# Eight experts on one core: a 64-column expert instead of a 128-column one behind the alternating pair

## The chip, the cores and the metric

The kernel runs on one core of one Trainium2 chip, as one launch. The metric is the device time of a run in microseconds (us). The kernel before was timed in three runs; one more execution was profiled, and all rows below are from that one.

## The reference

Two decoder layers over 256 positions of width 1024, all in float32. The first layer has a dense feed-forward part; the second, which this change is about, sends every position to 2 of 8 experts:

```
logits = x @ router_w                      # 256 x 8
top_val, top_idx = top_k(logits, 2)
comb = softmax(top_val), scattered to 8 columns
for e in range(8):
    h = silu(x @ w_gate[e]) * (x @ w_up[e])            # 1024 -> 3584
    y += comb[:, e:e+1] * (h @ w_down[e])              # 3584 -> 1024
x = layer_norm(ALPHA * x + y)
```

Each expert's three matrices are 1024 x 3584 (twice) and 3584 x 1024 in float32, 44 MB; all eight are read.

## The kernel before, in words

**Columns and positions.** The kernel doesn't run all 256 positions through each expert. It gathers an expert's positions with a one-hot matmul into a few columns (`start_expert`), and scatters the result back with the transposed one-hot (`finish_expert`). The experts come in eight *places*, called positions here, 0 to 7. Position 0 is expert 0 with 128 columns. The other seven experts are ranked at run time by how many positions chose them (rank 0 has most), and `SEQ[s]` says which rank comes at position s, `CAP[s]` how many columns it gets there: 128 for ranks 0 and 1, 64 for the others. What doesn't fit is done by a loop at the end that is skipped when nothing is left over. SyncE reads the expert's number from a register for each weight transfer, so the order is fixed in the program and the experts are chosen by data.

**Two kinds of expert.** `CAP[s] == P` decides how the weights are used (`moe_unit`, `moe_project`, `down_block`):
- A *wide* expert (128 columns): each weight unit is split after arrival into a high half by ScalarE (L125) and a low half by VectorE (L143), each into a ring of three buffers, and TensorE makes three float32r matmuls for each float32 product. The raw unit's buffer is free as soon as the low half is written.
- A *small* expert (64 columns): TensorE reads the raw float32 unit, with two groups of 64 columns side by side in the array. The raw unit's buffer is free when those matmuls are done (`U.done`).

**Blocks.** An expert has seven blocks of 512 hidden units. A block is two units for gate, two for up, and later two for down, of 1 MB each. `moe_project` makes gate, ScalarE applies silu (L1232), `moe_project` makes up, VectorE multiplies (L1242). The down projection of a block comes after the up projection of the next one, so gate, up and the earlier block's down share the stream's order. Positions 0 and 1 (wide and small) alternate block by block and are the *pair*; its last two blocks are (1,5) and (1,6), both small. From position 2 on the experts come one after the other. (2,0) is block 0 of position 2.

```
blocks = [(0, 0), (0, 1), (0, 2), (1, 0), (1, 1)]
blocks += [x for b in range(3, NB) for x in ((0, b), (1, b - 1))] + [(1, NB - 1)]
blocks += [(s, b) for s in range(2, E) for b in range(NB)]
```

**The stream.** All weights go through `WeightStream`, in the order of use, on SyncE's DMA queue (L104). A unit's transfer is issued when a buffer comes free (`_fill`, `_freed`); there are fourteen for raw units in this part (five from the start, four added, three tiles of the mixer, two taken from the rings). `U.next` and `U.raw` also start the splitting of wide units up to two units ahead (`LOOK = 2`).

Of the kernel before, what the change touches and what calls it, by code (L numbers as in the profile page):

```python
# [35 lines left out]
        "P10": 10, "P11": 0, "vt": 4, "Lh": 5, "Ll": 6, "PTa0": 7, "PTa1": 3, "O": 10, "Ah": 2, "Al": 1,  # L36
        "xT0": 6, "xT1": 7, "setup": 9, "xf0": 0, "xf1": 9}
NM2 = 3
SEQ = (None, 3, 0, 4, 1, 5, 2, 6)
CAP = (128, 64, 128, 64, 128, 64, 64, 64)  # L40
NW_BASE = 5
NW_EXTRA = 4
LOOK = 2
# [155 lines left out]
def trunk(ctx, tc, x, xT, w_in, w_out, prm, wbd, rb, ohc, cst, ln1_g, ln1_b, ln2_g, ln2_b,  # L199
# [77 lines left out]
    def moe_unit(w, s, b, half, k):  # L277
        def src():
# [3 lines left out]
            return w[ds(e, 1), b, half].rearrange("o p (k n) -> p (o k) n", k=k)  # L282
        units.append((src, (k, 2048 // k), None, CAP[s] == P))

# [759 lines left out]
    def one_hot(pool, posc, name, T=P, bufs=1):  # L1044
        oh = pool.tile([P, 2, P // T, T], F32, name=name, tag="oh", bufs=bufs)
        for t in range(2):
            V.tensor_scalar(oh[:, t], iota[:, None, 0:T].to_broadcast([P, P // T, T]), posc(t), None,
                            op0=ALU.is_equal)
        return oh

    def gather(oh, dst, T=P):
        n = 512 // T
        for q in range(KC // n):
            p = sm()[:, 0:n * T].rearrange("p (a b) -> p a b", a=n)
            for j in range(n):
                k = q * n + j
                for t in range(2):
                    mm(p[:, j, :], xt[t][:, k * P:(k + 1) * P], oh[:, t, 0, :], t == 0, t == 1)
            dst(slice(q * n, q * n + n), p)
# [30 lines left out]
    def expert_one_hot(s):  # L1090
        ohe[s] = one_hot(ep, lambda t: (pos if s == 0 else posq)[:, t, s:s + 1], f"oh{s}", CAP[s], 2)

    def start_expert(s):
        wide = CAP[s] == P
        g = [ep.tile([P, KC, CAP[s]], F32R if wide else F32, name=f"g{s}_{i}", tag="g", bufs=3)
             for i in range(1 + wide)]

        def dst(a, p):
            A.activation(g[0][:, a, :], p, AF.Copy)
            if wide:  # L1100
                V.tensor_tensor(out=g[1][:, a, :], in0=p, in1=g[0][:, a, :].bitcast(F32), op=ALU.subtract)  # L1101

        gather(ohe[s], dst, CAP[s])
        st[s] = g

    def moe_project(s, g, between=None):
        T_ = CAP[s]
        C = P // T_
        n = 512 // C
        p = sm()[:, 0:n]  # L1110
        for kh in range(2):
            if C == 1:
                wh, wl = U.next()
            else:
                i, w = U.raw()
            if kh == 1 and between is not None:
                between()
            for k in range(4):
                kk = kh * 4 + k
                if C == 1:  # L1120
                    mm(p, g[0][:, kk, :], wh[:, k, :], kk == 0, False)
                    mm(p, g[0][:, kk, :], wl[:, k, :], False, False)
                    mm(p, g[1][:, kk, :], wh[:, k, :], False, kk == KC - 1)
                    continue
                for c in range(C):
                    mm(p[c * T_:(c + 1) * T_, :], g[0][:, kk, :], w[:, k, c * n:(c + 1) * n], kk == 0, kk == KC - 1)
            if C > 1:
                U.done(i)
        return p
# [48 lines left out]
    def route_ranks():  # L1178
# [8 lines left out]
        for s in range(1, E):  # L1187
            V.tensor_scalar(perm[:, s - 1, :], rank7, float(SEQ[s]), None, op0=ALU.is_equal)
        V.tensor_scalar(id7, iota[:, 1:E], UNSEL, None, op0=ALU.add)
# [259 lines left out]
```

## Time and profile before

| | us |
|---|---|
| median of three runs | 1282.12 (1280.95 to 1283.67) |
| the profiled execution, device time | 1284.04 |
| its span, first to last instruction | 1282.3 |
| TensorE busy | 1224.8 |
| VectorE busy | 647.4 |
| ScalarE busy | 518.1 |

The span and the busy times come from the profile of one execution. A busy TensorE is not one at its peak, since the ends of pipelined matmuls are modelled. Engines: PE is TensorE (PEld its weight loads), DVE VectorE, ACT ScalarE, POOL GpSimd, SP SyncE, whose queue (SPq) issues the weight transfers. A row of a table of stretches gives the stretch, its length, the busy time (and instructions) of PE, PEld, DVE, ACT and POOL, the granted TensorE clock (1.00 is full), the busy share of the DMA engines, and GB/s. A row of the timeline gives start, duration, engine, line, operation, and in brackets the idle time before it and what ended it. A row of instructions of one tile gives durations in ns (least, median, most) and the first and last start in us. The experts of the second layer run from about 420 us to the end.

### The profile page before, as it was taken

Reading aid. Unit: us, or ns where it says so; the run is one execution under the profiler, and the core shown is the slowest. Engines: PE = TensorE matmul, PEld = TensorE weight load, DVE = VectorE, ACT = ScalarE, POOL = GpSimd, SP = SyncE. Lnnn points to the kernel's source line nnn. Section 1 sums busy time; section 2 is a strip of 40 time slices with the busy share of each in tenths; the row PEclk is TensorE's granted clock in tenths of the full one; section 3 lists DMA queues with packets and bytes.
Section 4 is the critical chain, followed back from the end, with each engine's and each line's share of the span. In section 5 each row is a group of like instructions: output and inputs, shape, how many; then the busy total and the mean of one; then the engine's idle time right before and its main releaser. Section 6 shows DMA issues by size and latency. Waiting matters only on the chain. (4 is left out here: it accounts for less than half of the span.)

```text
span 1282.3 us, 18541 instructions
## 1 busy us (share of the span) xinstructions
PE 1224.8 (96%) x7564; PEld 911.7 (71%) x7564; DVE 647.4 (50%) x616; ACT 518.1 (40%) x549; POOL 81.0 (6%) x75
## 2 busy tenths in 40 slices
PE   9999999999999899999999999999999999799884
PEld 8979999999987776666678875568886554354441
DVE  6597544457688753445588841069882001001004
ACT  5674443344683542444467731057762000000001
POOL 3124000004022010000000000000000000000001
PEclk9999999999999999999999999999999999999998
DMA  9843545554377769999999979999999999999994
GB/s 350 310 176 143 208 176 196 198 213 150 149 285 276 272 249 415 420 421 420 421 420 414 367 278 420 420 420 421 421 421 392 420 420 421 420 420 420 421 420 180
DMA packets 63506, 428.99 MB, mean 335 GB/s; under 512 B 7951, under 2 KB 8376, under 8 KB 12984
## 3 DMA queue, kind: packets, MB, share of 16 engines
q1 hardware_dynamic: 62408, 423.55, 81.8%
q0 software_dynamic: 720, 3.68, 0.8%
q8 instruction: 61, 1.00, 0.3%
q10 hardware_dynamic: 288, 0.52, 0.1%
q14 instruction: 29, 0.24, 0.0%
HBM read 426.67 MB, written 2.63 MB: 335 GB/s over the span
## 5 line engine op out<-in xcount | busy, mean ns | idle before, releaser
L143 DVE TENSOR_TENSOR lo<-w,hi 128x2048 fp32r<-128x2048 f32 (+1 forms) x181 | 402.6, 2242 | 88.5 <-ACT hi L125 87.4
L125 ACT ACTIVATE hi<-w 128x2048 fp32r<-128x2048 f32 (+1 forms) x183 | 340.6, 1875 | 92.3 <-PE sm L240 52.8
L240 PE MATMUL sm<-w,g 128*64 128x256 f32 x2240 | 265.8, 382 | 4.3 <-DMA w<-in_moe_w_up_dram 4.2
L240 PEld LDWEIGHTS sm<-w,g 128*64 128x64 f32 x2240 | 159.2, 137 | 100.2 <-issue 23.7
L240 PE MATMUL sm<-hi,g 128*128 128x512 f32 x672 | 220.8, 400 | 1.5 <-DVE g L1101 1.5
L1242 DVE TENSOR_TENSOR h<-h,sm 128x256 f32<-128x256 f32 (+1 forms) x56 | 29.0, 518 | 294.7 <-PE sm L240 290.3
L240 PE MATMUL acc<-w,ht 128*64 128x512 f32 x560 | 141.5, 603 | 20.3 <-DMA w<-in_moe_w_down_dram 19.7
L1140 ACT ACTIVATE ht<-sm 128x256 f32<-128x256 f32 (+1 forms) x56 | 25.6, 457 | 322.4 <-PE sm L1138 322.4
L240 PEld LDWEIGHTS sm<-hi,g 128*128 128x128 f32 x672 | 126.7, 189 | 33.4 <-DVE g L1101 2.0
L240 PE MATMUL sm<-lo,g 128*128 128x512 f32 x336 | 133.7, 398 | 3.3 <-DVE lo L143 3.3
L240 PE MATMUL sm<-xh,hi 128*128 128x256 f32 x528 | 132.5, 284 | 0.0
L240 PE MATMUL sm<-xl,hi 128*128 128x256 f32 x528 | 132.0, 283 | 0.0
L240 PEld LDWEIGHTS acc<-w,ht 128*64 128x64 f32 x560 | 40.8, 138 | 99.2 <-issue 70.3
L240 PE MATMUL acc<-hi,ht 128*128 128x512 f32 x336 | 109.8, 398 | 0.0
L240 PEld LDWEIGHTS sm<-xh,hi 128*128 128x128 f32 x528 | 99.6, 189 | 1.7 <-issue 1.3
L240 PEld LDWEIGHTS sm<-xl,hi 128*128 128x128 f32 x528 | 99.8, 189 | 0.4
L240 PE MATMUL sm<-xh,lo 128*128 128x256 f32 x528 | 84.8, 283 | 0.0
L240 PEld LDWEIGHTS sm<-lo,g 128*128 128x128 f32 x336 | 63.5, 189 | 18.4 <-DVE lo L143 4.3
L240 PEld LDWEIGHTS acc<-hi,ht 128*128 128x128 f32 x336 | 63.0, 187 | 17.3 <-issue 2.7
L240 PEld LDWEIGHTS sm<-xh,lo 128*128 128x128 f32 x528 | 72.3, 189 | 0.0
L240 PE MATMUL acc<-lo,ht 128*128 128x512 f32 x168 | 67.1, 400 | 5.1 <-DVE lo L143 5.1
L353 POOL TENSOR_TENSOR mv<-mv,mhalf 128x1 f32<-128x1 f32 x8 | 7.0, 877 | 815.4 <-DVE mv L352 815.4
(263 smaller groups left out, 1177.7 us busy)
## 6 DMA issues: line engine op xcount, KB each, us to landing
w<-in_moe_w_gate_dram SPq DMA_DIRECT2D x112, 1024.0 KB, 13.7
w<-in_moe_w_up_dram SPq DMA_DIRECT2D x112, 1024.0 KB, 14.3
w<-in_moe_w_down_dram SPq DMA_DIRECT2D x110, 1024.0 KB, 15.7
w<-in_w_in_dram SPq DMA_DIRECT2D x18, 1024.0 KB, 6.1
w<-in_ffn_w_gate_dram SPq DMA_DIRECT2D x11, 1024.0 KB, 4.8
w<-in_ffn_w_up_dram SPq DMA_DIRECT2D x11, 1024.0 KB, 5.7
w<-in_ffn_w_down_dram SPq DMA_DIRECT2D x11, 1024.0 KB, 6.1
w<-in_w_out_dram SPq DMA_DIRECT2D x8, 1024.0 KB, 4.8
```

The source lines that it names most:

```text
L125: self.nc.scalar.activation(hi[a], w[a], AF.Copy)
L143: V.tensor_tensor(out=lo[a], in0=w[a], in1=hi[a].bitcast(F32), op=ALU.subtract)
L240: T.matmul(o, l, r, start=first, stop=last)
L353: G.tensor_tensor(out=o, in0=o, in1=mhalf, op=ALU.pow)
L1140: A.activation(ht[0], p[:, 0:nj, :], AF.Copy)
L1242: V.tensor_tensor(out=h, in0=h, in1=pu, op=ALU.mult)
```

## The change

Two of the constants at the head of the kernel are edited. Positions 0, 1, 6 and 7 keep their ranks; positions 2 to 5 hold ranks 4, 0, 5, 1 (64, 128, 64, 128 columns) where they held ranks 0, 4, 1, 5 (128, 64, 128, 64 columns). No other line changes.

```
-SEQ = (None, 3, 0, 4, 1, 5, 2, 6)
-CAP = (128, 64, 128, 64, 128, 64, 64, 64)
+SEQ = (None, 3, 4, 0, 5, 1, 2, 6)
+CAP = (128, 64, 64, 128, 64, 128, 64, 64)
```

## Rows read from the trace of the kernel before

**Rows 1.** The page: GB/s in 40 equal slices; the largest group of DMA issues.

```profile
GB/s 350 310 176 143 208 176 196 198 213 150 149 285 276 272 249 415 420 421 420 421 420 414 367 278 420 420 420 421 421 421 392 420 420 421 420 420 420 421 420 180
...
w<-in_moe_w_gate_dram SPq DMA_DIRECT2D x112, 1024.0 KB, 13.7
```

**Rows 2.** Busy times by stretch: the pair; the small experts at positions 6 and 7.

```profile
500.00:640.00 140.00, 137.09 (x777) 92.83 (x777) 69.81 (x50) 58.77 (x50) 0.00 (x0) 1.00 1.01 420
...
1062.00:1250.00 188.00, 166.44 (x1100) 84.27 (x1098) 15.17 (x30) 12.98 (x31) 0.00 (x0) 0.99 1.01 420
```

**Rows 3.** Busy times by stretches of 20 us, the five below 400 GB/s.

```profile
700.00:720.00 20.00, 20.00 (x90) 16.10 (x89) 17.13 (x9) 14.40 (x9) 0.00 (x0) 1.00 0.97 379
720.00:740.00 20.00, 20.00 (x92) 16.16 (x91) 17.16 (x9) 14.39 (x10) 0.00 (x0) 1.00 0.96 366
740.00:760.00 20.00, 20.00 (x120) 15.82 (x120) 8.77 (x6) 6.00 (x7) 0.00 (x0) 1.00 0.64 241
760.00:780.00 20.00, 19.27 (x136) 12.52 (x134) 8.09 (x9) 5.95 (x7) 0.00 (x0) 1.00 0.93 378
...
960.00:980.00 20.00, 19.27 (x128) 14.09 (x128) 6.47 (x6) 5.18 (x5) 0.00 (x0) 1.00 0.94 374
```

**Rows 4.** Waits of SyncE's queue, 710 to 785 us: total us, times, longest.

```profile
SPq L104 <- DVE lo L143: 36.0, 15, 4.0
SPq L104 <- PE sm L240: 16.2, 5, 9.0
```

**Rows 5.** Issue and landing of the last up unit of (1,6), (3,6), (7,4).

```profile
L104 SPq DMA_DIRECT2D w<-in_moe_w_up_dram x1: 333/333/333, 586.2 to 586.2; - x1
...
DMA to landing us min/median/max: 16.5/16.5/16.5
...
L104 SPq DMA_DIRECT2D w<-in_moe_w_up_dram x1: 332/332/332, 810.2 to 810.2; - x1
...
DMA to landing us min/median/max: 18.2/18.2/18.2
...
L104 SPq DMA_DIRECT2D w<-in_moe_w_up_dram x1: 333/333/333, 1201.6 to 1201.6; - x1
...
DMA to landing us min/median/max: 19.8/19.8/19.8
```

**Rows 6.** Timeline of VectorE: the product of gate and up in ten blocks.

```profile
623.29 0.42 DVE L1242 TENSOR_TENSOR h<-h,sm 128x256 f32<-128x256 f32 x1 [2.00 <-PE sm L240]
...
748.28 0.68 DVE L1242 TENSOR_TENSOR h<-h,sm 128x512 f32<-128x512 f32 x1
...
767.07 0.41 DVE L1242 TENSOR_TENSOR h<-h,sm 128x256 f32<-128x256 f32 x1
...
835.42 0.42 DVE L1242 TENSOR_TENSOR h<-h,sm 128x256 f32<-128x256 f32 x1 [10.44 <-PE sm L240]
...
855.43 0.69 DVE L1242 TENSOR_TENSOR h<-h,sm 128x512 f32<-128x512 f32 x1 [4.44 <-ACT hi L125]
...
960.27 0.68 DVE L1242 TENSOR_TENSOR h<-h,sm 128x512 f32<-128x512 f32 x1
...
979.06 0.41 DVE L1242 TENSOR_TENSOR h<-h,sm 128x256 f32<-128x256 f32 x1
...
1047.38 0.42 DVE L1242 TENSOR_TENSOR h<-h,sm 128x256 f32<-128x256 f32 x1 [10.44 <-PE sm L240]
...
1062.10 0.42 DVE L1242 TENSOR_TENSOR h<-h,sm 128x256 f32<-128x256 f32 x1 [14.30 <-PE sm L240]
...
1223.47 0.42 DVE L1242 TENSOR_TENSOR h<-h,sm 128x256 f32<-128x256 f32 x1 [7.53 <-PE sm L240]
```

**Rows 7.** Groups by line and shape: the split of a wide unit (busy, mean ns).

```profile
L143 DVE TENSOR_TENSOR lo<-w,hi 128x2048 fp32r<-128x2048 f32 x175 | 397.3, 2289 | 86.2 <-ACT hi L125 85.2
L125 ACT ACTIVATE hi<-w 128x2048 fp32r<-128x2048 f32 x177 | 335.9, 1913 | 90.0 <-PE sm L240 52.8 <-PE acc L240 26.9 <-ACT hi L125 4.7
```

**Rows 8.** Busy times and granted clock, 1226 to 1230 us.

```profile
1226.00:1230.00 4.00, 3.61 (x10) 1.15 (x12) 0.00 (x0) 0.00 (x0) 0.00 (x0) 0.57 1.02 424
```

## The prediction

> **What bounds the kernel now.** I read the page's line of transfer rates first. From about 500 us to the end the weights of the experts arrive at 420 GB/s, slice after slice, and only three slices fall clearly below it: 367, 278 and, later, 392 [rows 1]. A block of an expert takes six units of 1024 KB [rows 1], 6.29 MB, so the stream needs 14.95 us for a block at 421 GB/s. The table by stages says that two different things go on under the same rate. From 500 to 640 us TensorE is busy 137.1 of 140 us, so it only just keeps step. From 1062 to 1250 us it is busy 166.4 of 188 us at the same 420 GB/s: it has caught up and waits for weights [rows 2]. The end of the kernel is therefore set by the stream: time is won only where the stream itself stands still, or after its last unit.
>
> Where does it stand still? In four windows from 700 to 780 us it moves 379, 366, 241 and 378 GB/s, and 374 in the window 960 to 980 [rows 3]. Against 420.5 the first four are short by 41.5, 54.5, 179.5 and 42.5, together 318 GB/s over 20 us, or 318 / 420.5 x 20 = 15.1 us of stream time. The last is short by 46.5, or 2.2 us. Sum 17.3 us. The list of waits of the issuing queue says why: from 710 to 785 us it waits 36.0 us for low halves on VectorE and 16.2 us for matmuls, once 9.0 us [rows 4]. Both are the last readers of a weight buffer. No buffer is free, because TensorE is too far behind the stream.
>
> **How far behind, block by block.** I call *lag* the time from the arrival of a block's fourth unit (the last of gate and up) to the product of gate and up on VectorE (L1242). Arrivals are issue plus time to landing [rows 5], products are in [rows 6].
> The last block of the pair: 623.29 - (586.2 + 16.5) = 20.6 us.
> The last block of position 3: 835.42 - (810.2 + 18.2) = 7.0 us.
> A block that has caught up: 1223.47 - (1201.6 + 19.8) = 2.1 us, which is the floor.
> A block changes the lag by its own duration less 14.95 us of stream:
> - A wide expert behind a small one: from 835.42 to 960.27, 124.85 us for seven blocks, less 104.65, adds 20.2 us.
> - The first small block behind a wide one (it carries the wide expert's last down projection): 979.06 - 960.27 = 18.79 (767.07 - 748.28 at the first place is the same), adds 3.8 us.
> - The six other blocks of a small expert: 1047.38 - 979.06 = 68.32, less 89.7, takes off 21.4 us.
> - The first small block behind a small one: 1062.10 - 1047.38 = 14.72, takes off 0.2 us.
>
> So before: 20.6 + 20.2 + 3.8 = 44.6 at the start of position 3, where the stream lost 15.1; what it bore was 29.5 us. At the start of position 5: 7.0 + 20.2 + 3.8 = 31.0, lost 2.2; what it bore was 28.8 us. The two places agree: with the buffers that there are, about 29 us of lag is free and each us beyond it stops the stream for a us.
>
> **The change part by part.** The two edited tuples send the same experts, with the same widths, through the same code in another order. Ranks 3, 4, 5, 2, 6 keep 64 columns and ranks 0, 1 keep 128, so no instruction of the expert blocks is added or removed, nor of the routing (four ranks and four capacities of it are other constants), nor bytes. The list of joints stays too: behind the pair before there come wide, small, wide, small, small, small; after small, wide, small, wide, small, small. Both have two joints small to wide, two wide to small and two small to small. All of this costs 0. What is moved is when the lag is high:
> - Position 2, now small, starts from the same 20.6: less 0.2 and 21.4 would be -1.0, so it ends at the floor, 2.1.
> - Position 3, wide: 2.1 + 20.2 = 22.3; the first block of position 4: 26.1. Below 28.8: the stream loses 0 where it lost 15.1.
> - The rest of position 4, small: 4.7. Position 5, wide: 24.9; the first block of position 6: 28.7. Just at the limit: it loses 0 to 0.7 where it lost 2.2. I take 0.7, because the limit is known to about that.
> - Position 6: 7.3. Position 7: less 0.2 and 21.4, so caught up again before the end, as it is before; the tail behind the last unit is the same.
>
> Two bounds have to be set that no row shows directly. First, no wide expert of the trace starts from a TensorE that has caught up. A wide unit needs its high half (1.913 us) and its low half (2.289 us) after arrival [rows 7], 4.2 us more than a small one, so the floor of its first block is 2.1 + 4.2 = 6.3. The measured step into a wide expert, 855.43 - 835.42 - 14.95 = 5.1 [rows 6], already brings the lag to 7.2, above that floor. So I add nothing; if the 4.2 came on top, the two peaks would be 30.3 and, from 28.8 - 21.4 = 7.4, 31.4, and the stream would lose 1.5 + 2.6 = 4.1. Second, the small expert behind the pair keeps its raw units until TensorE has read them, where a wide one gives its buffer back after the low half; but it comes at lag 20.6, and even small blocks bear 28.8: 0.
> Waits that the order brings: in the last block of position 2 TensorE waits for weights, with nothing behind it that the end depends on. The g buffers (three, a wide expert takes two) are asked for when the expert that held them is over in both orders: 0. The DMAs are the same units in the same queue; those of positions 2 to 5 are only of other experts.
>
> Sum: 17.3 - 0.7 = 16.6 us off. The profiled execution took 1284.04 us (span 1282.3 us) and would take 1267.4. The median of the runs shown is 1282.12, 1.9 below it, so I predict 1282.1 - 16.6 = **1265.5 us**. The bounds: with the 4.1 us lost, 13.2 us off, 1268.9. At the other end, from the arrival at 602.7 to that of the caught-up block 40 blocks later (1201.6 + 19.8 = 1221.4 [rows 5]) 618.7 us pass where 40 blocks at 14.95 would take 598.0: 20.7 us is all that the stream lost, late arrivals at full rate among it, and 1261.4 is the best time.
>
> **The rivals.**
> *A, the stall only moves.* It goes to the starts of positions 4 and 6 because a wide expert started cold adds more than 20.2 us. For it: the second peak, 28.7, has no reserve. Against: the same step was 20.2 from a lag of 7.0 and 124.99 us (from 623.29 to 748.28 [rows 6]) from 20.6, so it does not depend on the lag. With 4 us more at each start the peaks are 30.1 and 35.4, so 1.3 and 6.6 us are lost, 9.4 us are left of the gain, and the time is 1272.7; with 6 us more it is 1276.7.
> *B, nothing changes.* The stream's pause at 700 to 780 us would belong to that stretch and not to the order. Against it: the second wide expert, which came behind a small one, lost 2.2 instead of 15.1. Time 1282.
> *C, slower, by TensorE's clock.* A TensorE that has caught up waits, and after such waits the granted clock was 0.57 over 1226 to 1230 us [rows 8], which is a stretch of it at 1.2 GHz. If that came at the end of position 2 and stayed, a wide block of 124.85 / 7 = 17.8 us would take 35.7, 20.7 longer than the stream. The room of 28.8 - 2.1 = 26.7 hides one such block; to end above 1282 it must eat that room and the 16.6 us, more than two wide blocks at half clock. Against it: from 1062 to 1250 us TensorE waits in every block and the mean granted clock is 0.99 [rows 2]. The Trainium skill ("TensorE: Matmul & The Clock Gate", HAM oscillation) warns that a matmul loop that waits for each weight tile falls back to the slow clock every time, which speaks against this change. The trace does not bear that out for waits as short as these; by the rule every caught-up block would run at half rate, and position 2 would not catch up. If two such wide blocks and a half did, the time would be about 1290.
>
> **How the numbers follow.** The forecast gets 0.84, A 0.09, B 0.04, C 0.03. The forecast's own bounds are 1261.4 and 1268.9. For eight in ten I leave out B, C and the far part of A and cut the best end, which needs every late arrival to vanish: 1262.0 to 1271.5. Within 0.2% (2.6 us, about the spread of the runs, 1280.95 to 1283.67) is B; faster is the forecast and A, 0.93; same 0.04; slower 0.03.
>
> **What would show it.** In the changed profile: no window below 415 GB/s from 640 to 1040 us; TensorE waiting for weights in the last block or two of position 2, up to about 710 us (arrival 602.7 + 7 x 14.95 + 2.1); 128-column blocks from there to about 834 (602.7 + 14 x 14.95 + 22.3), and again from about 921 to 1046; at most a small dip at about 1050 to 1075 us, behind the second wide expert; no long wait of the issuing queue for matmuls before that; and the last unit some 16 us earlier, with the same tail. It is wrong if a deep dip stands again behind the first wide expert, at about 835 us (A), or still at 740 to 760 us (B), or if the clock's row shows half rate at the start of position 3 (C).

## The result, and the profile after

The changed kernel took 1267.51 us (median of four runs, 1266.41 to 1268.51) beside 1281.94 for the kernel before (four runs, one more than the prediction had): a ratio of 0.9886, 95% interval 0.9869 to 0.9903, or 14.4 us less. The forecast was 1265.5 us, with a range of 1262.0 to 1271.5; of the 16.6 us that it promised, 14.4 came. Run once more beside the experiments, the same kernel gave 0.9900 (0.9881 to 0.9919).

A second ruler, beside the time of a whole run, is one row of each trace: the first and the last start of the product of gate and up (56 blocks). First the kernel before, then the changed one (durations in ns, then the first and last start in us):

```profile
L1242 DVE TENSOR_TENSOR h<-h,sm x56: 412/422/689, 433.2 to 1253.3; 128x256 f32<-128x256 f32 x35, 128x512 f32<-128x512 f32 x21
```

```profile
L1242 DVE TENSOR_TENSOR h<-h,sm x56: 411/422/689, 431.8 to 1236.0; 128x256 f32<-128x256 f32 x35, 128x512 f32<-128x512 f32 x21
```

From block to block it is 820.1 us before and 804.2 after (804.5 in the second profile of the changed kernel): 15.9 less. The table below calls this the *stretch of the blocks*. Of the 15.9, 1.3 us lie ahead of the pair's last product (623.29 - 433.2 = 190.1 and 620.58 - 431.8 = 188.8), in blocks that the change doesn't touch; the kernel before with its second swap alone has 188.8 there too. So a difference of 1.3 us between two stretches is not yet an effect of an edit. Behind the pair's last product it is 630.0 us before and 615.4 after: 14.6 less.

The page of the changed kernel, its span and its line of transfer rates, answers to [rows 1]:

```profile
span 1265.4 us, 18541 instructions
...
GB/s 344 308 197 143 200 186 200 200 198 152 164 244 324 237 266 398 421 420 421 420 420 420 420 421 421 420 408 418 420 421 420 421 420 398 420 420 420 420 420 169
```

The hole of two slices (367, 278) is gone. What is left are two shallow places, 408 and 398. The windows of 20 us, as in [rows 3], say where (columns as there; the last is GB/s, the third from last the granted clock):

```profile
700.00:720.00 20.00, 17.51 (x119) 10.87 (x116) 6.01 (x5) 7.04 (x7) 0.00 (x0) 0.98 1.01 419
720.00:740.00 20.00, 20.00 (x86) 14.06 (x85) 13.48 (x10) 11.93 (x10) 0.00 (x0) 0.93 1.01 419
...
840.00:860.00 20.00, 19.27 (x124) 13.22 (x124) 6.54 (x6) 5.18 (x5) 0.00 (x0) 1.00 0.99 396
...
1040.00:1060.00 20.00, 20.00 (x122) 15.78 (x123) 8.46 (x6) 5.66 (x6) 0.00 (x0) 1.00 1.01 413
1060.00:1080.00 20.00, 19.27 (x134) 12.36 (x132) 8.27 (x9) 5.95 (x7) 0.00 (x0) 1.00 0.97 393
```

Three windows are short of 420.5 by 24.5, 7.5 and 27.5 GB/s, together 59.5 / 420.5 x 20 = 2.8 us of stream. Before it was 17.3 us. The difference, 14.5 us, is the 14.6 that the trace gained behind the pair, and the 14.4 by which the medians of the runs differ. (The spans of the two traces differ by more, 1282.3 - 1265.4 = 16.9 us: the kernel before was profiled in a run 2 us above its median.)

The timeline of VectorE at L1242, as in [rows 6], for the blocks (1,6), (2,6), (3,0), (3,6), (4,0), (4,6), (5,0), (5,6), (6,0):

```profile
620.58 0.42 DVE L1242 TENSOR_TENSOR h<-h,sm 128x256 f32<-128x256 f32 x1 [2.00 <-PE sm L240]
...
708.17 0.42 DVE L1242 TENSOR_TENSOR h<-h,sm 128x256 f32<-128x256 f32 x1 [13.71 <-PE sm L240]
...
731.06 0.69 DVE L1242 TENSOR_TENSOR h<-h,sm 128x512 f32<-128x512 f32 x1 [4.91 <-PE sm L240]
...
835.93 0.68 DVE L1242 TENSOR_TENSOR h<-h,sm 128x512 f32<-128x512 f32 x1
...
854.72 0.41 DVE L1242 TENSOR_TENSOR h<-h,sm 128x256 f32<-128x256 f32 x1
...
923.08 0.42 DVE L1242 TENSOR_TENSOR h<-h,sm 128x256 f32<-128x256 f32 x1 [10.44 <-PE sm L240]
...
943.09 0.69 DVE L1242 TENSOR_TENSOR h<-h,sm 128x512 f32<-128x512 f32 x1 [4.44 <-PE sm L240]
...
1047.93 0.68 DVE L1242 TENSOR_TENSOR h<-h,sm 128x512 f32<-128x512 f32 x1
...
1066.72 0.41 DVE L1242 TENSOR_TENSOR h<-h,sm 128x256 f32<-128x256 f32 x1
```

And the issue and landing of the third unit of (4,0) and of the fourth of (6,0), as in [rows 5]:

```profile
L104 SPq DMA_DIRECT2D w<-in_moe_w_up_dram x1: 333/333/333, 804.4 to 804.4; - x1
...
DMA to landing us min/median/max: 18.7/18.7/18.7
...
L104 SPq DMA_DIRECT2D w<-in_moe_w_up_dram x1: 333/333/333, 1019.2 to 1019.2; - x1
...
DMA to landing us min/median/max: 18.0/18.0/18.0
```

The unit at 804.4 lands at 823.1 and is the third of (4,0). The trace has no landing of the fourth; if it follows a unit (2.5 us) later, the first peak of the lag is 854.72 - 825.6 = 29.1 us. The row at 1019.2 is the fourth unit of (6,0), so the second peak is 1066.72 - 1037.2 = 29.5. The forecast had 26.1 and 28.7. The list of waits of the issuing queue from 840 to 880 us shows that the first peak does touch the limit, which the forecast had excluded:

```profile
SPq L104 <- PE sm L240: 20.3, 8, 9.0
```

It waits once 9.0 us for a matmul, as long as before. But the stream lost only 24.5 / 420.5 x 20 = 1.2 us there. The unit issued at 804.4 landed 18.7 us later, so about seven units of 2.5 us are on their way at a time and go on arriving during such a wait.

### The profile page after: what moved, and what is told of

It reads as the page before. It is cut to its first block, busy times and chain, and to the rows that moved or that the text cites. A ratio compares the mean times of both kernels' runs of the same rounds, so it can differ in the third digit from the quotient of the medians.

```text
span 1265.4 us, 18541 instructions
## 1 busy us (share of the span) xinstructions
PE 1217.8 (96%) x7564; PEld 908.8 (72%) x7564; DVE 647.6 (51%) x616; ACT 518.5 (41%) x549; POOL 82.0 (6%) x75
## 5 line engine op out<-in xcount | busy, mean ns | idle before, releaser
L240 PE MATMUL sm<-w,g 128*64 128x256 f32 x2240 | 261.6, 382 | 2.6 <-DMA w<-in_moe_w_up_dram 2.4
L1242 DVE TENSOR_TENSOR h<-h,sm 128x256 f32<-128x256 f32 (+1 forms) x56 | 29.0, 518 | 275.2 <-PE sm L240 275.2
L240 PE MATMUL acc<-w,ht 128*64 128x512 f32 x560 | 134.5, 596 | 11.6 <-DMA w<-in_moe_w_down_dram 11.0
L240 PEld LDWEIGHTS sm<-lo,g 128*128 128x128 f32 x336 | 63.4, 189 | 20.2 <-DVE lo L143 6.1
L240 PEld LDWEIGHTS acc<-hi,ht 128*128 128x128 f32 x336 | 63.0, 187 | 17.2 <-issue 2.7
## 6 DMA issues: line engine op xcount, KB each, us to landing
w<-in_moe_w_gate_dram SPq DMA_DIRECT2D x112, 1024.0 KB, 16.6
w<-in_moe_w_up_dram SPq DMA_DIRECT2D x112, 1024.0 KB, 17.2
```

Source lines behind the costliest of these rows:

```text
L240: T.matmul(o, l, r, start=first, stop=last)
L1242: V.tensor_tensor(out=h, in0=h, in1=pu, op=ALU.mult)
```

## The experiments

All ratios are to the kernel before, run beside them on the same chip. In these runs the kernel before measured 1283.3 to 1283.5 us (1281.94 beside the changed kernel's first four runs), so ratios are compared, not times. The stretch of the blocks comes from one profile of each kernel. An edit shifts line numbers: the product L1242 is L1243, L1244 or L1249 in some of them.

| run | ratio, 95% interval | stretch of the blocks, us |
|---|---|---|
| before | 1 | 820.1 |
| changed | 0.9886 (0.9869 to 0.9903) | 804.2 |
| changed, again | 0.9900 (0.9881 to 0.9919) | 804.5 |
| first swap alone | 1.0042 (1.0026 to 1.0057) | 824.6 |
| second swap alone | 0.9992 (0.9977 to 1.0008) | 818.1 |
| before, two of three gate and up matmuls | 0.9883 (0.9865 to 0.9901) | 804.3 |
| changed, one buffer fewer | 0.9896 (0.9877 to 0.9915) | 810.7 |
| before, one buffer fewer | 1.0009 (0.9998 to 1.0021) | 821.2 |
| changed, one buffer more for a low half | 0.9888 (0.9871 to 0.9904) | 806.1 |
| before, one buffer more for a low half | 1.0012 (1.0000 to 1.0025) | 822.9 |
| changed, clock kept up | 0.9881 (0.9863 to 0.9898) | 803.2 |
| changed, wide experts one position later | 0.9898 (0.9879 to 0.9916) | 810.9 |
| changed, positions 2 to 5 alternating | 0.9934 (0.9917 to 0.9950) | 811.7 |

The theory: the stream stops when TensorE is more than about 29 us behind it at the first small block after a wide expert, and the order decides how far behind it gets. First rival: what counts is merely that a small expert follows the pair. Second rival: VectorE's pace in making low halves, the largest sum of the queue's waits in [rows 4], is what holds the stream.

**Each swap alone.** The first swap puts a small expert behind the pair and leaves the two wide ones side by side; the second parts the wide ones and leaves a wide one behind the pair. The edits are against the changed kernel.

```
-SEQ = (None, 3, 4, 0, 5, 1, 2, 6)
-CAP = (128, 64, 64, 128, 64, 128, 64, 64)
+SEQ = (None, 3, 4, 0, 1, 5, 2, 6)          # first swap alone
+CAP = (128, 64, 64, 128, 128, 64, 64, 64)
+SEQ = (None, 3, 0, 4, 5, 1, 2, 6)          # second swap alone
+CAP = (128, 64, 128, 64, 64, 128, 64, 64)
```

> Only the first of the two swaps: behind the pair small, wide, wide, small, small, small. Theory (room of about 29 us of lag, wide adds 20.2, small takes off 21.4): the first wide ends at a lag of 25.3, the second at 45.5, the small block behind it at 49.3; the stream loses 20 us, so about 1284.6 us (1283 to 1287), no better than before, although a small expert follows the pair. Rival (what counts is that a small expert follows the pair): about 1267.5, as with both swaps.

> Only the second swap: behind the pair wide, small, small, wide, small, small. Theory: the first wide loses its 15.1 us as before, the second starts caught up, peaks at about 29 and loses 0 to 1.2 where it lost 2.2: about 1280.9 us (1279.5 to 1282). Rival (the two wide experts need only be further apart): clearly under 1277.

The first swap alone made the kernel slower, by 0.42% (a little more than expected: 1.0042 x 1281.94 is 1287.3 us), so the first rival falls: a small expert does follow the pair there. Its table of stretches (last column GB/s):

```profile
860.00:880.00 20.00, 20.00 (x91) 16.02 (x90) 19.05 (x14) 15.05 (x11) 0.00 (x0) 1.00 0.98 390
...
880.00:1000.00 120.00, 119.27 (x606) 91.01 (x604) 83.05 (x54) 66.16 (x48) 0.00 (x0) 1.00 0.89 348
```

Against 420.5 this is 1.5 and 20.7 us, 22.1 us lost in one hole that begins within the second wide expert and ends behind it, where 20 was expected. The second swap alone:

```profile
640.00:760.00 120.00, 120.00 (x580) 94.13 (x579) 95.44 (x60) 76.28 (x53) 0.00 (x0) 1.00 0.93 373
760.00:880.00 120.00, 117.73 (x835) 65.02 (x831) 17.55 (x30) 10.92 (x24) 0.00 (x0) 1.00 1.00 413
...
1000.00:1120.00 120.00, 119.27 (x680) 84.94 (x680) 64.68 (x46) 51.81 (x42) 0.00 (x0) 1.00 1.01 417
```

It keeps the hole behind the pair (13.6 + 2.1 us) and loses 1.0 at the second wide expert; its ratio is what was expected. So neither swap gains by itself: with one, the two wide experts add 40 us of lag in a row, with the other the first one adds 20 to the 20 that the pair leaves. Only both together keep each wide expert's 24 us inside the room.

**TensorE's pace or VectorE's.** The kernel before, with the wide experts at positions 2 and 4 leaving out the matmul of the low half of x (part of the product is missing); the splits on ScalarE and VectorE stay.

```
-                mm(p, g[0][:, kk, :], wl[:, k, :], False, False)
-                mm(p, g[1][:, kk, :], wh[:, k, :], False, kk == KC - 1)
+                mm(p, g[0][:, kk, :], wl[:, k, :], False, s > 1 and kk == KC - 1)
+                if s < 2:
+                    mm(p, g[1][:, kk, :], wh[:, k, :], False, kk == KC - 1)
```

> The kernel before; the wide experts at positions 2 and 4 leave out one of the three matmuls of gate and up (low half of x times high half of the weights), so 56 of 72 matmuls a block; the splits on ScalarE and VectorE stay. Theory (TensorE's pace makes the lag): a wide block falls from 17.2 to about 15 us, the lag stays near 29, the stream loses 0 to 2 us instead of 17.3: about 1265 us. Rival (VectorE's pace of low halves, the longest wait of the queue before, makes it): the splits are as slow as before, 1280 or more.

In the old order, with every split still made, the gain is as large as the change's. Two products of position 2, and the stretch around them:

```profile
719.88 0.68 DVE L1243 TENSOR_TENSOR h<-h,sm 128x512 f32<-128x512 f32 x1
...
734.85 0.68 DVE L1243 TENSOR_TENSOR h<-h,sm 128x512 f32<-128x512 f32 x1
```

```profile
680.00:740.00 60.00, 57.70 (x263) 44.29 (x262) 54.03 (x33) 43.81 (x31) 0.00 (x0) 1.00 1.01 421
```

A wide block falls to 14.97 us, the stream's own pace, and the stream runs at 421 GB/s from 680 to 740 us, where it fell to 379 and 366. So it was TensorE's 17.2 us, and the second rival falls. VectorE is not far behind, busy 54.0 of 60 us here; what would hold a wide block next was not tried.

**Room: one buffer fewer, in both kernels.** `NW_EXTRA = 3` instead of 4.

> The changed kernel with one raw weight buffer fewer (thirteen). Theory: a buffer is 2.49 us of stream, both peaks stand at the limit, so each loses 2.5 us more: about 1272.5 us (plus up to 2.5 if the filling of the buffers ahead of the experts loses one unit as well). Rival (the stream is not held by the room but by the pace of the engines that split or multiply): no change, 1267.5.

> The kernel before with one raw weight buffer fewer (thirteen). Theory: both places where it loses are past the limit, so 2 x 2.49 us more: about 1286.9 us (plus up to 2.5 for the filling ahead of the experts). Rival (pace, not room): no change, 1281.9.

In the changed kernel both dips get deeper, but by less than expected. These are the windows at its two peaks, 396 and 393 GB/s with fourteen buffers:

```profile
840.00:860.00 20.00, 19.27 (x134) 14.31 (x133) 7.00 (x5) 5.18 (x5) 0.00 (x0) 1.00 0.92 357
...
1060.00:1080.00 20.00, 19.27 (x133) 12.76 (x133) 6.54 (x6) 5.56 (x6) 0.00 (x0) 1.00 0.94 371
```

They lose 3.0 and 2.4 us, where with fourteen buffers the first peak lost 1.2 and the second 1.7 (1040 to 1080 us): 2.5 more together, one buffer's worth, where 5.0 was expected. Its stretch of the blocks is 6.5 us longer, but this is the profile of the slowest of four runs (1277.26 us; the others 1269.47 to 1272.68), and the timed ratio moved by only 0.001, within both intervals: the runs alone don't settle the size. The kernel before was a miss: it was to lose 5 us, and lost at most 2.7 by its interval and 1.1 by its stretch. Its rates and the end of its pair:

```profile
640.00:760.00 120.00, 120.00 (x575) 94.03 (x575) 94.72 (x59) 75.40 (x53) 0.00 (x0) 1.00 0.93 373
760.00:880.00 120.00, 118.47 (x744) 74.35 (x741) 48.57 (x43) 37.84 (x38) 0.00 (x0) 1.00 1.00 413
```

```profile
L104 SPq DMA_DIRECT2D w<-in_moe_w_up_dram x1: 332/332/332, 586.7 to 586.7; - x1
...
DMA to landing us min/median/max: 16.2/16.2/16.2
```

```profile
620.98 0.42 DVE L1242 TENSOR_TENSOR h<-h,sm 128x256 f32<-128x256 f32 x1 [1.99 <-PE sm L240]
```

The pair leaves a lag of 620.98 - 602.9 = 18.1 us here, 2.5 less than 20.6. With one more buffer (the experiment below, in the kernel before) the same unit is issued at 583.4 us, lands 16.6 later, and its product starts at 622.84: a lag of 22.8. So the lag behind the pair goes with the number of buffers, 18.1, 20.6 and 22.8 us for thirteen, fourteen and fifteen. The likely reason is that the buffers hold the stream up to about 480 us (249 to 285 GB/s in [rows 1]), and that from there the pair only keeps step. One buffer fewer lowers room and lag alike, and the loss behind the pair stays what it was. The changed kernel's dips fit this: the first wide expert starts from the floor of 2.1, which no buffer changes, and loses 1.8 us more; the second starts from what the first peak leaves, which falls with the room, and loses only 0.7 more. So a buffer counts once for the two peaks, and not at each.

**Room: one buffer more.** No buffer is added: one of the three buffers for low halves becomes a raw buffer, and low halves are made one unit ahead instead of two.

```
+    def next_two_lo(self):
+        w = self.next(1)
+        self.ahead_hi(2)
+        return w
...
-                wh, wl = U.next()
+                wh, wl = U.next_two_lo()
...
-    U.ahead(3)
+    U.shrink(0, 1)
+    U.ahead(2)
+    U.ahead_hi(3)
```

> The changed kernel with one of the three ring buffers of low halves given to the raw units (fifteen raw buffers, two low halves; a wide unit's low half is now made one unit ahead, its high half still two). Theory: a raw buffer is 2.49 us of room, so the two places where the stream still loses, 2.9 us together, lose nothing, and the filling ahead of the pair gains up to 2.5 us: 1262 to 1265 us, with wide blocks still at 17.2 us. Rival (a low half made one unit ahead is late, so wide blocks grow to 18 us or more): each wide expert adds 5 us or more to the lag, which eats the room: 1268 or more.

> The kernel before with the same exchange of a low-half buffer for a fifteenth raw buffer. Theory, as corrected by the run with thirteen: the lag with which the pair ends rises with the room, so the loss of 15.1 us at position 3 and of 2.2 at position 5 stays, and only the filling ahead of the pair gains, about 2.5 us: about 0.998 of the kernel before. Rival (each place where it loses gains the buffer's 2.5 us): 0.994 or less. If wide blocks grow, slower than before by 5 us or more.

Neither gained, so both expectations missed, and the stretches grew by 1.9 and 2.8 us. The pair's last product already comes later: 622.84 - 431.6 = 191.2 us after the first one in the kernel before, where the kernels above have 188.8 to 190.1. The last two products of position 3 and the first of position 4 in the changed order show what it costs behind the pair:

```profile
819.35 0.69 DVE L1249 TENSOR_TENSOR h<-h,sm 128x512 f32<-128x512 f32 x1 [0.68 <-PE sm L245]
...
836.78 0.69 DVE L1249 TENSOR_TENSOR h<-h,sm 128x512 f32<-128x512 f32 x1 [0.68 <-PE sm L245]
...
856.93 0.41 DVE L1249 TENSOR_TENSOR h<-h,sm 128x256 f32<-128x256 f32 x1
```

A wide block now takes 17.43 us instead of 17.22. The 20.15 us of the small block behind it, instead of 18.79, are not a loss of TensorE: without the buffer's change VectorE makes the product of (3,6) late, behind a split, and here it waits for TensorE instead (0.68 us in the row). From the product of (3,0), at 731.13, to that of (4,0) it is 125.80 us instead of 854.72 - 731.06 = 123.66: a wide expert costs 2.1 us more, most of the 2.49 that a buffer gives. That the low half, made later, is the reason is likely but not shown. These two runs change room and pace together and prove nothing about the room alone.

**The start of a wide expert from a TensorE that has caught up.** Six matmuls of constants ahead of block (3,0), into a tile that nothing reads.

```
+        if (s, b) == (3, 0):
+            keep_warm(6, sm())
```

> The changed kernel with six matmuls of constants, which nothing reads, ahead of the first matmuls of position 3, where TensorE waits 1.8 us for the first low half. Theory: the first block of position 3 took 22.89 us instead of the 20.0 of a wide start that has some lag, 1.0 of it more wait and about 1.7 the clock's fall for 3.4 us at 719 us; with the clock kept up, the block takes about 21.2 us and the first small dip (840 to 860 us) gets smaller; the time falls by 0 to 1.2 us. Rival (the cost of a cold start is the wait for the split alone): 22.9 us and the same dip.

In the changed kernel, TensorE at that place and its clock just after:

```profile
715.62 0.49 PE L240 MATMUL sm<-hi,g 128*128 128x512 f32 x1 [0.21 <-ACT hi L125]
717.95 0.50 PE L240 MATMUL sm<-lo,g 128*128 128x512 f32 x1 [1.83 <-DVE lo L143]
```

```profile
719.00:723.00 4.00, 4.00 (x13) 3.13 (x12) 3.67 (x2) 2.74 (x2) 0.00 (x0) 0.57 0.99 414
```

With the six matmuls, the products of (2,6) and (3,0), the clock, and the window of the first dip:

```profile
708.59 0.42 DVE L1244 TENSOR_TENSOR h<-h,sm 128x256 f32<-128x256 f32 x1 [13.73 <-PE sm L240]
...
729.81 0.69 DVE L1244 TENSOR_TENSOR h<-h,sm 128x512 f32<-128x512 f32 x1 [4.03 <-PE sm L240]
```

```profile
719.00:723.00 4.00, 4.00 (x19) 3.18 (x19) 3.79 (x2) 3.34 (x2) 0.00 (x0) 1.00 1.02 424
...
840.00:860.00 20.00, 19.27 (x129) 12.88 (x129) 6.54 (x6) 5.56 (x6) 0.00 (x0) 1.00 1.01 411
```

The block takes 21.22 us instead of 731.06 - 708.17 = 22.89, the granted clock stays at 1.00 instead of 0.57, and the first dip is 411 GB/s instead of 396, so 0.5 us instead of 1.2. The stretch of the blocks is 1.0 us shorter. The fall of the clock is no accident of one profile: the second profile of the changed kernel and that of the first swap alone both have 0.66 over 720 to 725 us. The rival, that the wait for the split is all, falls: 1.7 us of the 2.9 that a cold start cost were the clock. In the timed runs the kernel can't be told from the changed one (0.9881 beside 0.9886 and 0.9900).

**The wide experts one position later.** `SEQ = (None, 3, 4, 5, 0, 2, 1, 6)`, `CAP = (128, 64, 64, 64, 128, 64, 128, 64)`.

> Both wide experts one position later: behind the pair small, small, wide, small, wide, small. Theory: two small experts take off no more than one, since the lag can't fall below 2.1; the peaks are 29 and 30, loss about 3, but only one small expert is left behind the last wide one, so the kernel ends with a lag of about 7.5 instead of 2.1: about 1273 us. Rival (a longer stretch of small experts ahead of the wide ones gives more reserve): 1264 to 1267.

Issue and landing of the last block's fourth unit, and its product:

```profile
L104 SPq DMA_DIRECT2D w<-in_moe_w_up_dram x1: 333/333/333, 1219.1 to 1219.1; - x1
...
DMA to landing us min/median/max: 17.8/17.8/17.8
```

```profile
1244.37 0.42 DVE L1242 TENSOR_TENSOR h<-h,sm 128x256 f32<-128x256 f32 x1 [10.44 <-PE sm L240]
```

The last block ends with a lag of 1244.37 - 1236.9 = 7.5 us, as expected, and a second small expert ahead of the wide ones gave nothing. The price was over-estimated: the stretch is 6.7 us longer, but the end of the kernel follows 1270.2 - 1244.4 = 25.8 us behind the last product instead of 29.4, since most of the last down weights have landed by then. Together 3.1 us in the profiles; by the ratios it can't be told from the changed kernel.

**Alternating blocks.** A try for a still faster version: positions 2 and 3, then 4 and 5, go block by block, the small one first.

```
-    blocks += [(s, b) for s in range(2, E) for b in range(NB)]
+    blocks += [(s + i, b) for s in (2, 4) for b in range(NB) for i in range(2)]
+    blocks += [(s, b) for s in (6, 7) for b in range(NB)]
... (one-hot matrices: three buffers, made at other blocks)
```

> The changed kernel's experts in the changed order, but positions 2 and 3, and then 4 and 5, alternate block by block (small first), as the pair does; the one-hot matrices get three buffers instead of two and are made at other blocks. Theory: a wide and a small block together take 28.1 us, less than two blocks of stream, so the lag never leaves 20 to 29 and the remaining loss of 2.9 us goes: about 1264.6 us. Rival (changing between the kinds of expert costs TensorE time at every block): 1267.5 or more.

It was 0.3 to 0.5% slower than the changed kernel. Three products, (3,6), (4,0) and (5,0), and the rates behind them:

```profile
838.38 0.69 DVE L1243 TENSOR_TENSOR h<-h,sm 128x512 f32<-128x512 f32 x1 [4.45 <-PE sm L240]
...
857.85 0.41 DVE L1243 TENSOR_TENSOR h<-h,sm 128x256 f32<-128x256 f32 x1
...
877.72 0.69 DVE L1243 TENSOR_TENSOR h<-h,sm 128x512 f32<-128x512 f32 x1 [3.39 <-PE sm L240]
```

```profile
860.00:880.00 20.00, 20.00 (x90) 14.77 (x91) 13.93 (x12) 8.74 (x8) 0.00 (x0) 1.00 0.91 376
880.00:900.00 20.00, 19.28 (x117) 12.86 (x114) 12.46 (x9) 10.42 (x8) 0.00 (x0) 1.00 0.87 342
```

My arithmetic left out the joint: starting two experts in a row takes 19.5 and 19.9 us, 9.4 us more than the stream, while an alternating pair of blocks gives back only half a us (14.34 + 15.09 against 29.9; the products of (3,2), (2,3) and (3,3) start at 720.65, 734.99 and 750.08). The expectation had 28.1 for such a pair, so the rival, that changing between the kinds costs time at every block, holds in part. The lag never comes down from the pair's level, and the second joint goes over the limit. Sequential experts are better here because a whole small expert takes off 21 us before the next joint.

## Why the prediction was right, and where it was off

- *The stream's pauses set the time.* Right. Lost stream went from 17.3 to 2.8 us, the time from 1281.94 to 1267.51.
- *The room of about 29 us.* Right as a limit, to about a us: the first wide expert's peak of 29.1 lost 1.2, so 27.9 us were borne there. From that the steps of the prediction make the second peak 27.9 - 21.4 + 20.2 + 3.8 = 30.5; it lost 35 / 420.5 x 20 = 1.7 us, so 28.8 were borne. (The 29.5 above is less, since it counts from an arrival that was itself late: the fourth unit of (5,6) landed at 1021.1, and 1037.2 is 16.1 us behind it instead of 14.95.) What the text did not say is that the lag behind the pair hangs on the same buffers; the run with one fewer showed it. It did not touch the forecast, since the buffers didn't change.
- *The steps of the lag.* From a lag of some us the step into a wide expert is the same as before (943.09 - 923.08 = 20.01, as 855.43 - 835.42 in [rows 6]), and so is the first small block behind it (854.72 - 835.93 = 18.79). The small expert behind the pair did catch up: position 2 ends at 708.17, 87.6 us after the pair, where seven blocks of stream and a fall from 20.6 to 2.1 make 86.2.
- *The term that was mis-sized:* "So I add nothing" for a wide expert that starts from a TensorE that has caught up. It took 22.89 us, 2.9 more than 20.0. With it the first peak is 29.1 instead of 26.1, which touches the limit; and the second starts from that. By the prediction's own steps the two peaks then lose 29.1 - 21.4 + 24.0 - 28.8 = 2.9 us together; measured were 2.8, where 0.7 had been forecast. So this one term accounts for the miss. The bound that I set beside it (4.2 us on top, 4.1 us lost, 1268.9) held. The run with the clock kept up shows 1.7 of the 2.9; the rest, about 1.2, fits the longer wait for the first low half (1.83 us, where the trace of the kernel before has 0.81 ahead of (4,0)) but was not tried by itself.
- *Rival C* was right in its mechanism and wrong in its size. The clock did fall to half at the start of position 3, for a few us, and did not stay there. The caught-up blocks at the end, where TensorE waits in every block, keep a granted clock of 1.00:

```profile
1160.00:1180.00 20.00, 18.41 (x120) 8.79 (x118) 2.54 (x5) 0.77 (x2) 0.00 (x0) 1.00 1.01 420
1180.00:1200.00 20.00, 17.54 (x118) 8.58 (x116) 0.85 (x2) 1.15 (x3) 0.00 (x0) 1.00 1.01 421
1200.00:1220.00 20.00, 17.39 (x126) 9.04 (x122) 0.42 (x1) 1.15 (x3) 0.00 (x0) 1.00 1.01 420
```

The Trainium skill ("TensorE: Matmul & The Clock Gate", HAM oscillation) describes a loop that falls back to the slow clock at every tile, and there the wait for a tile is longer than the computing on it. In these rows the longest wait of TensorE is 1.5 us in blocks of 14.95, so this trace doesn't contradict the page; the prediction's "every caught-up block would run at half rate" asked more of the rule than the page says. The one fall, 0.57 over 719 to 723 us, came after waits of TensorE of at most 1.83 us.

- *Rival A* was right in its mechanism too: a wide expert that starts cold adds more than 20.2 us, and a small stall did move to both places. Its size was wrong: 2.9 us at the first start only and not 4 or 6 at both, so the peaks lost 2.8 us together instead of 8 or 12.
- *Rival B* fell: the hole was a matter of order, as the two swaps alone show.
- *What would show it:* the window 840 to 860 us at 396 GB/s is under the 415 that I had set as the least.

## What to carry to other kernels

Where a weight stream sets the time, as here, keep an account of how far the compute is behind it, block by block: pieces that are slower than the stream add to it, quicker ones take off, and only what goes over the buffers' room costs time. Sort the pieces so that each slow one starts from a low lag; half of such a reordering can be worth nothing, or less. A piece that starts from a fully caught-up engine can pay more than one with some work waiting (2.9 us here), so leave that in the sum.

## What the runs showed of the hardware that was not expected

- TensorE's granted clock fell to half for a few us where it passed from waiting for weights to waiting for the first split unit (0.57 over 719 to 723 us), and six constant matmuls in that wait kept it at 1.00. That was worth 1.7 us of one block.
- Where the issuing queue waited 9.0 us for a buffer (840 to 880 us of the changed kernel) the stream lost only 1.2 us, since about seven units were on their way. Such waits in the profile are not stalls of the stream by themselves; the GB/s of the window is what to read.
- The lag with which the pair ends followed the number of raw buffers: 18.1, 20.6 and 22.8 us for thirteen, fourteen and fifteen.
